# Forty-eight weight copies change their issuing engine, and one tile its place in a round of four

## The chip, the cores and the metric

The kernel runs on one core of a Trainium2 chip. The metric is the device time of one execution, in microseconds (us). Five engines work beside each other on a core, each with its own queue of instructions, done in order: TensorE (PE; PEld is its loading of weights), VectorE (DVE), ScalarE (ACT), GpSimd (POOL) and the sync engine (SP), which computes nothing and issues transfers. ACT and POOL can issue transfers too.

## The reference

A transformer trunk of two layers over 512 tokens of width 1024, all in float32:

```python
for layer in range(2):
    hn = rmsnorm(h, norm_mix[layer])
    if layer == 0: h = h + hybrid_attention(hn, ...)         # 8 grouped-query heads and 8 latent heads
    else:          h = h + neighbourhood_attention(hn, ...)  # 16 heads, an 8 x 16 window, a learned bias
    h = h + sq_relu_mlp(rmsnorm(h, norm_ffn[layer]), ffn_w_up[layer], ffn_w_down[layer])
return rmsnorm(h, final_norm)

def sq_relu_mlp(h, w_up, w_down):     # w_up 1024 x 4096, w_down 4096 x 1024
    u = relu(h @ w_up)
    return (u * u) @ w_down
```

## The kernel before

**Products.** Every float32 operand is split into a high part, rounded to a format that TensorE multiplies at its higher rate (`F32R`), and the rest, the low part. A product is three matmuls: high x high, high x low, low x high (`mm3`, L545 to L547). A weight chunk of 128 x 1024 is loaded by SP into half a raw tile (L214), ACT writes its high part `whi` (L236), and DVE the low part `wlo` (L226). `whi` and `wlo` have three buffers each. Chunks are loaded some 5 or 7 ahead of their use (`LOAD`) and split 2 ahead (`AHEAD`).

**The order of work.** The program is written as one stream. A planner then orders each engine's queue, by its own estimated times and with the place in the stream as priority; the order is fixed before the run. Three things bind it. `tc.keep_in_program_order(x)` puts `x` behind the instruction of the same engine that was written just before it. Inside `fixed_order()` (the second layer's attention) PE, ACT, DVE and POOL keep the written order, SP does not. And an instruction that must wait for data or for a free buffer holds up all that is behind it in its queue.

**The MLP.** `mlp_swept(l, made)` begins with `first_product`. It normalises `h`: for each of 8 blocks `hT[k]`, ACT and DVE write the high and low part of the scaled block (`split_g`, L551 and L552) and add its square to a sum (`sumsq_acc`, L559 on ACT, L561 on DVE). The first six tiles of `h @ w_up` are plain products: chunks 0 to 3 for four tiles, chunks 4 and 5 for two. The row norms are not needed before these end up in PSUM, so the norm's own matmuls (`compact_r`, L566) stand some steps into the product: after step 11 in the first layer, 13 in the second. Six chunks of `w_down` follow, and then the rest of `h @ w_up` by a scheme of seven products in place of eight for blocks of 2 x 2 (`Seven`, L416 to L418), whose weight sums POOL makes (`seven_chunk`, L326 to L331) and whose tiles are split at L336 and L337. The second product of the MLP goes by such a scheme as well (`Sweeps`, L1331 to L1449).

**Sums made ahead.** The sweeps need sums of blocks of `w_down`. `SumsAhead` makes them in device memory while earlier stages run: for each of 13 (first layer) or 11 (second) pairs of rows it copies two blocks of 512 KB from the weights to `made` (L841, issued by ACT), and POOL then adds blocks onto them with four accumulating transfers of 256 KB (L832). `steps()` is a generator; `tick` takes a step of it every few microseconds of planned TensorE work, from the latter part of the first attention (L1163), from the start of the second one (L1838) and through the MLP (`beat["every"]`). At the end of the up product `drain()` takes what is left.

**Raw tiles and the shared tile.** There are three raw tiles of 128 x 2048 (tag `raw`). In the MLP a fourth takes turns with them: the first 2048 columns of `shared`, whose 2560 columns otherwise hold five probability tiles of the attention (`p_tile`, 512 columns each, used in turn; the fifth is also `acc`, the sum of squares). `raw_pair()` hands out the next tile, as two halves for two chunks, or whole for a pair of `Seven`. `wide[0]` counts the place in the round, and 0 switches the shared tile off:

```python
        if wide[0]:
            wide[0] = wide[0] % 4 + 1
            if wide[0] == 1:
                return shared[:, 0:2048]
```

Before each MLP the attention's output projection runs (`out_proj`); its last chunks, five k-tiles first and three more after the last head in the second layer, lie in raw tiles. In the attention of the second layer ACT and POOL make the probabilities in `shared` (L1733, L1703) and PE transposes them from there (L1725); L1745 is the product with the values, L1714 the scores with their bias, which SP loads per head (L1778). L1004 adds the projection's tiles to `hT`.

Of the kernel before, what the change touches and what calls it, by code (L numbers as in the profile page):

```python
# [35 lines left out]
def encoder_kernel(ctx: ExitStack, tc: tile.TileContext, ins, out, dbg=None):  # L36
    nc = tc.nc
    PE, ACT, DVE, POOL, SP = nc.tensor, nc.scalar, nc.vector, nc.gpsimd, nc.sync
# [153 lines left out]
    wide = [0]  # L192
# [63 lines left out]
    LOAD = [5]  # L256
# [83 lines left out]
    class Seven:  # L340
# [27 lines left out]
        def split(self, kp, held=lambda z: z):  # L368

            for b in range(7):  # L370
                i = self.number(kp, b) // 2
                if i not in self.slots:
                    self.slots[i] = Slot()
            raw, t = self.raw.pop(kp)
            r, t_ = (s_.t.rearrange("p (b n) -> p b n", n=256) for s_ in (raw, t))
            b = 0
            while b < 7:
                q = self.number(kp, b)
                n = 2 if b in (3, 5) or (b < 2 and q % 2 == 0) else 1
                s_ = r[:, 1 + b : 1 + b + n] if b < 3 else t_[:, b - 3 : b - 3 + n]  # L380
                if n == 1:
                    d = self.at(kp, b)
                    hi, lo, s_ = d[:, 0], d[:, 1], s_[:, 0]
                else:
                    q = self.number(kp, b)
                    d = self.slots[q // 2].t.rearrange("p (q z n) -> p q z n", q=2, z=2)
                    hi, lo = d[:, :, 0], d[:, :, 1]
                ACT.activation(hi, s_, AF.Copy)
                held(DVE.tensor_tensor(lo, s_, f32(hi), op=ALU.subtract))
                b += n  # L390
                yield
            raw.free()
            t.free()
# [99 lines left out]
    def tiles(c0, n):  # L493
        return [(c0 + o, min(P, n - o)) for o in range(0, n, P)]
# [44 lines left out]
    def drain():  # L539
        for _ in beat["work"]:  # L540
            pass
# [279 lines left out]
    class SumsAhead:  # L821
# [12 lines left out]
        def steps(self):  # L834
            for kp in range(self.n + 3):
                if kp > self.n:
                    yield
                    yield
                if kp < self.n:
                    for z in range(2):  # L840
                        tc.keep_in_program_order(ACT.dma_start(self.made[kp, z], self.w[kp, z]))  # L841
                        yield
                for back, to, src, of in ((1, (1, 1), (0, 1), self.w), (1, (0, 1), (0, 0), self.w),
                                          (2, (0, 0), (1, 1), None), (3, (1, 0), (0, 0), None)):
                    if 0 <= kp - back < self.n:
                        self.add(kp - back, to, src, of)
                        yield
# [443 lines left out]
    def bias_rows():  # L1291
        held = tc.keep_in_program_order
        slot = Slot(F32)
        R, Fi, Fe = (slot.t[:, a:b] for a, b in ((0, 248), (248, 624), (624, 1008)))
        rpb = ins["od_rpb"][0]
        for qr in range(8):
            held(SP.dma_start(R[16 * qr : 16 * qr + 16],
                              rpb.rearrange("h a b -> h (a b)")[:, (7 - qr) * 31 : (7 - qr) * 31 + 248]))
            yield
        held(POOL.memset(Fi, NEG))  # L1300
        held(POOL.memset(Fe[:, 256:384], NEG))
        rv = R.rearrange("p (k d) -> p d k", d=31)
        held(POOL.tensor_copy(Fi.rearrange("p (j k) -> p j k", k=8)[:, 15:31, :], rv[:, 7:23, :]))
        held(POOL.tensor_copy(Fe[:, 0:248].rearrange("p (j k) -> p j k", k=8), rv))
        yield
        bxv = bx.rearrange("h t (c r) k -> t c r h k", r=8)
        for c in range(16):
            held(SP.dma_start(bxv[0, c].rearrange("r h k -> r h k"), Fi[:, (15 - c) * 8 : (15 - c) * 8 + 256]))
            yield

            v, off = (1, (7 - c) * 8) if c < 8 else (0, (23 - c) * 8)
            held(SP.dma_start(bxv[1, c][:, :, 128 * v : 128 * v + 128], Fe[:, off : off + 128]))
            yield
            held(SP.dma_start(bxv[1, c][:, :, 128 - 128 * v : 256 - 128 * v], Fe[:, 256:384]))
            yield
        slot.free()
# [35 lines left out]
    class Sweeps:  # L1352
# [66 lines left out]
        def run(self, R):  # L1419
# [33 lines left out]
            starts = {(0, 0), (0, 1), (1, 0), (2, 1)}  # L1453
            tail, held, waiting = [], {}, []
            for i, (kind, kp) in enumerate(steps):
                if i + 1 < len(steps):
                    ready_[steps[i + 1]] = self.tokens(*steps[i + 1])
# [50 lines left out]

    def mlp_swept(l, made, last=None):

        wide[0], LOAD[0] = 4, 7
        beat["every"] = (3.3, 3.6)[l]
        stage, ahead, later = first_product(l)
        w = ins["ffn_w_down"][l]
        bias = bias_rows() if l == 0 else iter(())
        U = stage(FIRST)[0]
        up = [s_.pair() for s_ in U]

        def ev(m, b):
            DVE.tensor_tensor(hT[:, m, :], hT[:, m, :], b, op=ALU.add)  # L1520

        gens = [product(w, 0, up, tiles(512 * c, 512), lambda j, b, c=c: ev(4 * c + j, b)) for c in range(2)]
        ahead()
        for c, gen in enumerate(gens):
            for i, _ in enumerate(gen):
                later(c, i)
                if i % 4 == 3 and c * 6 + i // 4 < 10:
                    next(bias, None)
        for s_ in U:
            s_.free()  # L1530
        reserve[0] = 3
        beat["every"] = (5.4, 7.0)[l]
        sweeps = []

        R = stage(0, RAW[l] + MORE[l], 0, lambda: sweeps.append(Sweeps(w, FIRST, made)))[1]
        R, more = R[: RAW[l] // 2], R[RAW[l] // 2 :]
        V = [Slot() for _ in range(MORE[l])]

        def split_more():
            for n, v in enumerate(V):  # L1540
                raw = more[n // 2]
                split(raw.t[:, S * (n % 2) : S * (n % 2) + S], v.pair())
                if n % 2:
                    raw.free()
                yield

        rest = split_more()
        drain()
        wide[0], LOAD[0] = 0, 5
        spare.clear()  # L1550
        reserve[0] = 6
        if last:
            beside = last(FIRST + RAW[l], V)
        else:
            beside = lambda kind, kp: None
            up = [s_.pair() for s_ in V]
            gens = [product(w, FIRST + RAW[l], up, tiles(512 * c, 512), lambda j, b, c=c: ev(4 * c + j, b))
                    for c in range(2) if up]
        for n, (kind, kp) in enumerate(sweeps[0].run(R)):
            beside(kind, kp)  # L1560
            if n % 16 == 15:
                next(rest, None)
            if kind and n % 5 == 0:
                next(bias, None)
        assert all(next(x, 0) == 0 for x in (rest, bias))
        reserve[0] = 1
        if not last:
            flip[0] = 1
            for gen in gens:
                for _ in gen:  # L1570
                    pass
            for s_ in V:
                s_.free()

    mlp_swept(0, ahead0)


# [276 lines left out]
    def last_mlp():  # L1854
# [80 lines left out]
        def last(k0, tiles_):  # L1935
# [10 lines left out]
            return beside  # L1946

        mlp_swept(1, ahead1, last)
        flip[0] = 1
        for run in runs:  # L1950
# [57 lines left out]
```

## Time and profile before

| | us |
|---|---|
| runs | 1174.4, 1178.94, 1178.77 (median 1178.77) |
| the profiled execution's own time | 1176.78 |
| its span | 1175.0 |
| busy: PE / DVE / ACT / POOL | 1145.0 / 917.2 / 673.8 / 467.3 |
| mean granted TensorE clock | 0.995 of full speed |

A line of the timeline has the start in the span, the duration, the engine, the line of the kernel, the operation, the tiles (written <- read), the shape, a count where neighbours are merged, and in brackets how long the engine was idle before it and what it waited for. SPq, ACTq and POOLq are the issuing of transfers by these engines' queues. A line of the chain that ended last has start, duration, and the work or the transfer that the chain went through. A row of a table of waits has who waited for whom, the total in us, how often, and the longest. Transfers issued by SP are queue q1 in the page, by ACT q10, by POOL q0; a row has packets, MB, and the packets' time as a share of 16 DMA engines over the span.

### The profile page before, as it was taken

How to read it: one execution, taken by the hardware profiler on the slowest of the kernel's cores; microseconds unless marked ns; L12 is line 12 of the kernel's file. 1: busy time of each engine (PE TensorE's matmuls, PEld its weight loads, DVE VectorE, ACT ScalarE, POOL GpSimd, SP SyncE). 2: the span in 40 equal slices, each digit the busy share in tenths (PEclk: the TensorE clock that was granted, in tenths of full speed). 3: DMA queues.
4: the chain of work that ended last, by engine and by line, in shares of the span. 5: the costliest groups of instructions: out<-in, count | busy, mean ns of one | idle time of the engine just before them, and what ended most of it. 6: DMA issues, size and time to landing. Idle time of an engine off the chain costs nothing.

```text
span 1175.0 us, 21065 instructions
## 1 busy us (share of the span) xinstructions
PE 1145.0 (97%) x7668; PEld 1033.8 (88%) x7668; DVE 917.2 (78%) x1627; ACT 673.8 (57%) x1157; POOL 467.3 (40%) x494
## 2 busy tenths in 40 slices
PE   9989999999999999999999999999899999999997
PEld 8667778888899999999998998988688999999995
DVE  5798988878878888998485666667796878799855
ACT  5468577564536657557454556545452665675625
POOL 3267354343878884000002243342285788400000
PEclk9999999999999999999999999999899999999998
DMA  7122478893776647867536498789467544565702
GB/s 272 55 80 83 134 188 210 185 231 125 168 173 170 152 119 209 272 192 252 184 107 162 130 264 226 189 208 253 161 132 188 133 122 116 161 208 180 250 2 71
DMA packets 131752, 197.32 MB, mean 168 GB/s; under 512 B 13012, under 2 KB 81537, under 8 KB 130881
## 3 DMA queue, kind: packets, MB, share of 16 engines
q1 hardware_dynamic: 113232, 138.18, 37.6%
q0 software_dynamic: 16128, 31.48, 16.3%
q10 hardware_dynamic: 2288, 26.32, 6.5%
q8 instruction: 60, 0.98, 0.4%
q14 instruction: 44, 0.35, 0.1%
HBM read 173.52 MB, written 56.62 MB: 196 GB/s over the span
## 4 chain that ended last, share of the span: by engine, by line
PE 77%; DVE 5%; DMA 5%; issue 1%; ACT 0%; POOL 0%; SPq 0%; DVEq 0%; ACTq 0%; POOLq 0%
PE mm L547 6%; PE mm L545 6%; PE mm L546 6%; PE mm L418 3%; PE mm L416 3%; PE mm L417 3%; PE t L1443 3%; PE t L1445 3%; PE t L1444 3%; DMA a<-a 2%; PE mm L1445 2%; PE mm L1443 2%; PE t L416 2%; PE mm L1444 2%; PE t L417 2%; PE t L418 2%
## 5 line engine op out<-in xcount | busy, mean ns | idle before, releaser
L545 PE MATMUL mm<-a,whi 128*128 128x512 f32 x395 | 160.9, 409 | 3.7 <-ACT whi L236 1.9
L547 PE MATMUL mm<-a,wlo 128*128 128x512 f32 x395 | 156.7, 399 | 0.3 <-DVE wlo L226 0.3
L546 PE MATMUL mm<-a,whi 128*128 128x512 f32 x395 | 156.6, 396 | 0.1
L337 DVE TENSOR_TENSOR wlo<-raw,whi 128x896 fp32r<-128x896 f32 x80 | 109.8, 1377 | 27.9 <-ACT whi L336 27.3
L336 ACT ACTIVATE whi<-raw 128x896 fp32r<-128x896 f32 x80 | 75.5, 950 | 87.0 <-PE o L546 27.5
L236 ACT ACTIVATE whi<-raw 128x1024 fp32r<-128x1024 f32 (+3 forms) x82 | 76.3, 933 | 75.6 <-PE s L546 26.9
L226 DVE TENSOR_TENSOR wlo<-raw,whi 128x1024 fp32r<-128x1024 f32 (+4 forms) x79 | 94.3, 1195 | 30.7 <-ACT whi L236 30.4
L545 PEld LDWEIGHTS mm<-a,whi 128*128 128x128 f32 x395 | 74.8, 189 | 20.2 <-ACT whi L236 3.0
L547 PEld LDWEIGHTS mm<-a,wlo 128*128 128x128 f32 x395 | 74.9, 190 | 17.3 <-DVE wlo L226 1.1
L546 PEld LDWEIGHTS mm<-a,whi 128*128 128x128 f32 x395 | 74.9, 190 | 13.2 <-DVE a L588 0.4
L1341 DVE TENSOR_TENSOR wlo<-a,whi 128x1024 fp32r<-128x1024 f32 x54 | 66.4, 1232 | 25.1 <-ACT whi L1340 25.0
L1611 POOL DMA_DIRECT2D a<-a x16 | 8.6, 542 | 182.0 <-PE mm L547 167.2
L1443 PE MATMUL t<-a,whi 128*128 128x256 f32 x288 | 80.8, 281 | 0.0
L1444 PE MATMUL t<-a,whi 128*128 128x256 f32 x288 | 80.8, 280 | 0.0
L1445 PE MATMUL t<-a,wlo 128*128 128x256 f32 x288 | 80.7, 280 | 0.0
L1078 POOL TENSOR_SCALAR shared<-shared,ti 128x512 f32<-128x512 f32 x64 | 47.2, 741 | 84.0 <-DVE ti L1077 64.9
L418 PE MATMUL mm<-a,wlo 128*128 128x256 f32 x280 | 78.8, 281 | 1.0 <-DVE wlo L337 1.0
L417 PE MATMUL mm<-a,whi 128*128 128x256 f32 x280 | 78.5, 281 | 0.0
L416 PE MATMUL mm<-a,whi 128*128 128x256 f32 x280 | 78.4, 280 | 0.0
L1340 ACT ACTIVATE whi<-a 128x1024 fp32r<-128x1024 f32 x54 | 56.9, 1054 | 37.4 <-PE t L1444 30.4
L1703 POOL TENSOR_SCALAR shared<-shared,ti 128x256 f32<-128x256 f32 x64 | 34.7, 557 | 92.3 <-DVE ti L1702 79.8
L330 POOL TENSOR_TENSOR raw<-raw 128x512 f32<-128x512 f32 x40 | 63.0, 1575 | 3.1
(399 smaller groups left out, 4028.4 us busy)
## 6 DMA issues: line engine op xcount, KB each, us to landing
made<-in_ffn_w_down_dram ACTq DMA_DIRECT2D x48, 512.0 KB
a<-made SPq DMA_DIRECT2D x86, 256.0 KB
raw<-in_ffn_w_up_dram SPq DMA_DIRECT2D x80, 256.0 KB
made<-in_ffn_w_down_dram POOLq DMA_DIRECT2D x48, 256.0 KB, 5.9
made<-made POOLq DMA_DIRECT2D x48, 256.0 KB, 6.0
raw<-in_ffn_w_down_dram SPq DMA_DIRECT2D x32, 256.0 KB
a<-in_ffn_w_down_dram SPq DMA_DIRECT2D x32, 256.0 KB
raw<-in_od_w_qkv_dram SPq DMA_DIRECT2D x64, 128.0 KB
```

Of the source, the lines that this page charges most:

```text
L226: z = lambda: (eng or DVE).tensor_tensor(to, src, f32(high), op=ALU.subtract)
L236: ACT.activation(hi[:, 0:m], raw[:, 0:m], AF.Copy)
L337: DVE.tensor_tensor(lo[:, 0:896], raw[:, 128:1024], f32(hi[:, 0:896]), op=ALU.subtract)
L416: PE.matmul(o, wh, x[:, 0], start=kp == 0 and n in (0, 1, 3, 5), stop=False, skip_group_check=True)
L417: PE.matmul(o, wh, x[:, 1], start=False, stop=False, skip_group_check=True)
L418: PE.matmul(o, wl, x[:, 0], start=False, stop=kp == self.np - 1, skip_group_check=True)
L545: PE.matmul(o, wh, xh, start=first, stop=False)
L546: PE.matmul(o, wh, xl, start=False, stop=False)
L547: PE.matmul(o, wl, xh, start=False, stop=last)
L1443: PE.matmul(o, wh, x[:, 0], start=first and m % 2 == 0, stop=False, skip_group_check=True)
L1444: PE.matmul(o, wh, x[:, 1], start=False, stop=False, skip_group_check=True)
L1445: PE.matmul(o, wl, x[:, 0], start=False, stop=last, skip_group_check=True)
```

## The change

The copies to `made` are issued by SP instead of ACT. And `wide[0]` starts at 1 instead of 4 in each MLP, so that the counter gives 2, 3, 4 and then 1: the shared tile is handed out fourth in each round, not first. The number of tiles, the chunks and their order, and all arithmetic stay.

```diff
@@ SumsAhead.steps
                 if kp < self.n:
                     for z in range(2):
-                        tc.keep_in_program_order(ACT.dma_start(self.made[kp, z], self.w[kp, z]))
+                        tc.keep_in_program_order(SP.dma_start(self.made[kp, z], self.w[kp, z]))
                         yield
@@ mlp_swept
-        wide[0], LOAD[0] = 4, 7
+        wide[0], LOAD[0] = 1, 7
         beat["every"] = (3.3, 3.6)[l]
```

## Prediction

> **What bounds the kernel now.** I read the page first, then the table of busy time in 25 us stretches, then the chain that ended last where that table shows a hole, and around the hole the timelines of PE, ACT, DVE and SP.
>
> ```profile
> PE 1145.0 (97%) x7668; PEld 1033.8 (88%) x7668; DVE 917.2 (78%) x1627; ACT 673.8 (57%) x1157; POOL 467.3 (40%) x494
> ```
>
> TensorE is the bound: 30 us of 1175.0 are not PE time. An edit that adds or removes no matmul can win only where PE is idle, or where its clock is low.
>
> ```profile
> 775.00:800.00 25.00, 24.95 (x137) 21.14 (x136) 17.45 (x48) 12.23 (x33) 8.93 (x13) 1.00 0.82 226
> 800.00:825.00 25.00, 23.97 (x115) 19.00 (x114) 18.39 (x30) 13.33 (x22) 6.04 (x8) 1.00 1.02 272
> 825.00:850.00 25.00, 20.38 (x81) 16.38 (x80) 17.67 (x31) 9.52 (x15) 4.32 (x3) 0.86 0.40 139
> 850.00:875.00 25.00, 25.00 (x110) 20.36 (x109) 22.76 (x21) 17.57 (x30) 21.61 (x20) 1.00 0.63 137
> ```
>
> The first number behind the stretch's length is PE's busy time; the last three are granted clock, DMA share and GB/s. The hole lies at 823 us, where the second MLP begins. PE is idle for 50 - 23.97 - 20.38 = 5.65 us there, and the clock of 0.86 costs (1 - 0.86) x 25 = 3.5 us more. Just ahead of it the DMA engines are full (1.02). PE's timeline splits the hole in two:
>
> ```profile
> 823.96 0.50 PE L545 MATMUL mm<-a,whi 128*128 128x512 f32 x1 [0.83 <-ACT whi L236]
> 824.30 0.39 PE L546 MATMUL mm<-a,whi 128*128 128x512 f32 x1
> 824.53 0.39 PE L545 MATMUL mm<-a,whi 128*128 128x512 f32 x1
> ...
> 830.71 0.55 PE L566 MATMUL t<-ones,shared 128*128 128x1 f32 x3 [4.62 <-DVE shared L561]
> ```
>
> 0.83 us go on the high part of the first up-weight chunk (L236), 4.62 us on the last step of the sum of squares (L561), in all 5.45. Both lead back to one place on ACT:
>
> ```profile
> 817.96 0.61 ACT L559 ACTIVATE sc<-hT 128x512 f32<-128x512 f32 x1
> 822.85 2.01 ACT L236 ACTIVATE whi<-shared 128x1024 fp32r<-128x1024 f32 x2 [4.28 <-DMA shared<-in_ffn_w_up_dram]
> 824.76 0.71 ACT L551 ACTIVATE a<-hT,gT 128x512 fp32r<-128x512 f32 x1
> ...
> 828.77 0.61 ACT L559 ACTIVATE sc<-hT 128x512 f32<-128x512 f32 x1
> ```
>
> ACT waits 4.28 us for the load into `shared`, and behind it in ACT's order stand the four pairs L551/L559 that DVE's L552/L561 need. The chain shows why the load is late:
>
> ```profile
> 804.40 0.45 PE t L1725 x4
> ...
> 804.91 17.84 DMA shared<-in_ffn_w_up_dram
> ```
>
> SP may start it only when PE has transposed the last probabilities, which lie in the same tile; it then took 17.84 us, behind other transfers.
>
> **Edit 1: the shared tile comes fourth in the round (`wide[0]` 1 instead of 4).** `raw_pair` steps `wide[0]` before it tests it. So now the first pair of up chunks (0 and 1) takes `shared`, chunks 2 to 5 two raw tiles, down chunks 0 and 1 the third. After the edit chunks 0 to 5 take the three raw tiles, and down chunks 0 and 1 take `shared`. It is the same ring of four, shifted. SP's issues show when each tile came free:
>
> ```profile
> 798.62 0.37 SPq L214 DMA_DIRECT2D shared<-in_ffn_w_up_dram  x1
> 801.18 3.06 SPq L214 DMA_DIRECT2D raw<-in_ffn_w_up_dram  x3
> 804.91 0.37 SPq L214 DMA_DIRECT2D shared<-in_ffn_w_up_dram  x1
> 805.33 0.73 SPq L214 DMA_DIRECT2D raw<-in_ffn_w_up_dram  x1
> 813.31 4.50 SPq L214 DMA_DIRECT2D raw<-in_ffn_w_down_dram  x2
> ```
>
> The last two probability tiles of the attention are `shared[0:1024]`, the place of chunk 0, so 804.91 is chunk 0 and 798.62 is chunk 1. After the edit chunk 0 gets the raw tile of 801.18, 3.73 us earlier and ahead of the loads that now precede it. Even with the same 17.84 us it would land at 801.18 + 17.84 = 819.02. ACT's four earlier pairs end at 817.96 + 0.61 = 818.57, so L236 starts at about 819 at worst instead of 822.85, and PE, which ends the output projection at about 823.1, does not wait: 0.83 us gained.
>
> What is late next is the sum of squares. Its pairs need `hT`:
>
> ```profile
> 821.11 0.69 DVE L1004 TENSOR_TENSOR hT<-hT,s 128x512 f32<-128x512 f32 x1 [0.98 <-PE s L547]
> 821.80 1.38 DVE L1004 TENSOR_TENSOR hT<-hT,t 128x512 f32<-128x512 f32 x2
> 823.17 0.69 DVE L1004 TENSOR_TENSOR hT<-hT,o 128x512 f32<-128x512 f32 x1
> ...
> 829.97 0.69 DVE L561 TENSOR_TENSOR shared<-shared,sc 128x512 f32<-128x512 f32 x1
> ```
>
> The first is there at 821.80. ACT's four pairs, which now run from 824.76 to 829.38, can start about 2.9 us earlier, so the last L561 ends near 830.66 - 2.9 = 827.8. Meanwhile PE has work: the norm's matmuls (L566) stand after 14 steps of the product, each three matmuls at 0.23 us (the starts at 824.30 and 824.53), 14 x 0.69 = 9.7 us, until about 832.8. PE reached them early only because the low part of chunk 0 (L226) was missing and the planner put L566 ahead of L547. With L236 done by 820.1, DVE can do L226 in the 0.98 us ahead of 821.11 at the price of pushing L1004 by some tenths. So the 4.62 us go too. The first MLP has this picture already: its load into `shared` is no wait for ACT and PE has no gap there.
>
> With the gap the low clock goes:
>
> ```profile
> 73.75 0.73 PE L1070 MATMUL s<-a,a 128*128 128x512 f32 x2 [2.39 <-DVE ti L1074]
> ```
>
> This gap of 2.39 us left the clock at full speed, the one of 4.62 us did not; so any rest below 2.4 us keeps it. [...]
>
> Edit 1 gives 0.83 + 4.62 + 3.5 = 8.95 us. Its other effects I take at nothing. Chunks 4 and 5 are issued at 813.31 instead of 805.33; PE needs chunk 4 after four chunks of 8 x 0.69 = 5.5 us, at 823.1 + 22 = 845, so 17.84 us of landing fit, with 14 to spare. In the first MLP the ring moves in the same way, under PE that is never idle there. Bounds: 0 (the rivals) and 8.95.
>
> **Edit 2: 48 copies of 512 KB move from ACT's queue to SP's.**
>
> ```profile
> L841 ACTq DMA_DIRECT2D made<-in_ffn_w_down_dram x48: 496/496/852, 130.3 to 894.5; - x48
> ```
>
> ACT loses 48 x 0.496 = 23.8 us of issuing. ACT is 57% busy and, beyond the hole above, no PE gap from 210 us to the end is over 0.6 us, so I take this as 0. SP gains as much; it mostly waits. [...]
>
> What remains is order. A copy waits for no data; it is pinned only behind the SP transfer traced before it, and so goes out earlier than now rather than later, and may stand ahead of loads in one queue.
>
> ```profile
> q10 hardware_dynamic: 2288, 26.32, 6.5%
> ```
>
> ACT's queue (q10) moved 26.32 MB in 6.5% of the span, so one copy (0.524 MB) is 0.065 x 1175 x 0.524 / 26.32 = 1.5 us of all 16 engines. At the hole it matters like this:
>
> ```profile
> 811.95 0.50 ACTq L841 DMA_DIRECT2D made<-in_ffn_w_down_dram  x1
> ```
>
> Two copies issued there would go out before 801, ahead of chunk 0: at most 3.0 us, 819.0 + 3.0 = 822.0, still ahead of 823.1. In the first layer's attention five waits of the chain are for SBUF to SBUF transfers from SP, the first and the last of which are
>
> ```profile
> 141.16 5.50 DMA a<-a
> ...
> 205.40 5.67 DMA a<-a
> ```
>
> A copy in front of each would cost 5 x 1.5 = 7.5 us at most. At best the moves gain the 0.5 us that PE idles for them at 156.3. Copies stand among these transfers today as well (205.18 in the last wait), so I take half a copy: 0.8 us lost.
>
> **The sum.** 1176.78 - 8.95 + 0.8 = 1168.6 us against the profiled execution's own 1176.78 (span 1175.0). That execution lies 2.0 us below the median of 1178.77, inside the runs' 1174.4 to 1178.94. The mean of these four is 1177.2, and from there I get 1169.1; I say 1169.5.
>
> **Rivals.** First, the hole is shortened, not closed. If the planner leaves L226 behind the eight L552/L561, PE does eight matmuls (1.9 us) from 823.1 and waits from 825.0 to 827.8. Then 0.83 + 1.8 us are gained, and the clock's 3.5 us or not: 1171 to 1174.5. For it: that is DVE's order today. Against: today L236 comes so late that DVE had no other choice; in the first MLP L226 stands ahead of these.
>
> Second, edit 1 wins and edit 2 gives it back: the five transfers above each get a whole copy in front, 8.95 - 7.5 = 1.5 us left, 1175.3. For it: PE's order is fixed before the run, so a late transfer stalls it. Against: PE idles only 0.5 us for them now and has other work around.
>
> Third, slower: SP holds the copies up. SP issues in order, and a load that waits for its tile holds what is behind it:
>
> ```profile
> SPq L1778 <- DVE ti L1714: 55.5, 12, 10.8
> ```
>
> POOL's accumulating transfers (L832) wait for the copies, and POOL's scaling of the probabilities stands behind them:
>
> ```profile
> 679.91 0.50 ACTq L841 DMA_DIRECT2D made<-in_ffn_w_down_dram  x1
> ...
> 688.39 0.86 POOL L832 DMA_DIRECT2D made<-in_ffn_w_down_dram  x1
> ```
>
> The first pair has 8.5 us; later pairs have the planned two copies and up to four additions between. It decides when a copy comes over 8.5 - 1.5 = 7 us late. With waits of up to 10.8 us each stall costs up to 3.8 us; four of them, and edit 1 lost to the same queue, give 1176.8 + 15 = 1192; with edit 1 kept, 1183. Against it: a copy traced behind a load is mostly issued early, as SP runs ahead.
>
> **How the numbers follow.** Forecast 0.52, first rival 0.20, second 0.15, third 0.13. Half a per cent is about 5.9 us, what a measurement of this kernel can tell from no change; below 1172.9 is faster, above 1184.7 slower. Faster takes nine tenths of the forecast and a third of the first rival, 0.54; slower nearly all of the third rival, 0.12; the rest, 0.34, is the same. The likeliest case alone reaches from 1164 (runs that start at 1174.4, the full 8.95 and the 0.5 at 156 and a little of ACT's) to 1173. Taking in the second rival with some room for a few stalls of its kind, and leaving the third out, 1164 to 1181 leaves out about 0.18.
>
> **What would show it.** Right: around 815 to 830 us ACT's first L236 of the second MLP reads `raw`, with no wait for a DMA; L566 comes after some 14 steps, without a gap; the stretch after 825 has a clock of 1.00; DMA issues by ACT shrink to the constants and the output, and q10 to a few MB. Wrong: a PE gap over 2.4 us at the same place; new PE gaps at 140 to 215 us behind DMA a<-a; POOL's L832 waiting for `made`; in the first MLP a gap where up chunks 4 and 5 come late.

## The result and the profile after

The changed kernel takes 1167.52 us (median of 6 runs, 1165.67 to 1169.0), the kernel before beside it 1178.86 (6 runs, 1174.4 to 1182.38): a ratio of 0.9901, 95% interval 0.9883 to 0.992. It is faster by 11.3 us. The profiled execution took 1167.6, with a span of 1165.8; the one of before took 1176.78.

The page after, busy times and the two transfer queues of SP (q1) and ACT (q10):

```profile
PE 1141.2 (98%) x7668; PEld 1032.8 (89%) x7668; DVE 912.2 (78%) x1627; ACT 674.7 (58%) x1157; POOL 464.3 (40%) x494
...
q1 hardware_dynamic: 114768, 163.35, 43.6%
...
q10 hardware_dynamic: 752, 1.15, 0.4%
```

The 25 MB of copies have left ACT's queue; ACT's and POOL's busy times change by less than 1%. The table of stretches shows the hole at the start of the second MLP gone, with a clock of 1.00 where it was 0.86, and a new low clock at 50 to 100 us (1.00 in both stretches before):

```profile
50.00:75.00 25.00, 18.88 (x80) 12.43 (x79) 20.78 (x45) 13.57 (x25) 13.56 (x9) 0.98 0.36 110
75.00:100.00 25.00, 24.91 (x145) 20.43 (x143) 20.81 (x53) 19.86 (x45) 16.48 (x18) 0.95 0.16 37
800.00:825.00 25.00, 24.55 (x118) 19.83 (x117) 20.44 (x34) 15.30 (x28) 7.11 (x8) 1.00 1.03 282
825.00:850.00 25.00, 25.00 (x116) 20.56 (x115) 23.12 (x37) 12.32 (x21) 10.15 (x10) 1.00 0.29 91
```

The timeline of the changed kernel at the same place, ACT, DVE and PE:

```profile
819.23 1.04 ACT L236 ACTIVATE whi<-raw 128x1024 fp32r<-128x1024 f32 x1
...
820.21 0.68 DVE L561 TENSOR_TENSOR shared<-shared,sc 128x512 f32<-128x512 f32 x1
820.82 1.21 DVE L226 TENSOR_TENSOR wlo<-raw,whi 128x1024 fp32r<-128x1024 f32 x1
821.95 0.68 DVE L1004 TENSOR_TENSOR hT<-hT,s 128x512 f32<-128x512 f32 x1
...
829.01 0.68 DVE L561 TENSOR_TENSOR shared<-shared,sc 128x512 f32<-128x512 f32 x1
...
831.18 0.95 PE L566 MATMUL t<-ones,shared 128*128 128x1 f32 x8
```

ACT no longer waits for a load, and PE no longer waits at L566. But there is a third difference. DVE now takes the low part of chunk 0 (L226) ahead of the last four L1004. In the kernel before, DVE's timeline has it behind the last L561:

```profile
829.97 0.69 DVE L561 TENSOR_TENSOR shared<-shared,sc 128x512 f32<-128x512 f32 x1
830.57 2.36 DVE L226 TENSOR_TENSOR wlo<-shared,whi 128x1024 fp32r<-128x1024 f32 x2
```

In the prediction the early load brought the early L226. The experiments ask whether that is so.

### The profile page after: what moved, and what is told of

It is laid out like the page before. It is cut to its first block, busy times and chain, and to the rows that moved or that the text cites. A ratio compares the mean times of both kernels' runs of the same rounds, so it can differ in the third digit from the quotient of the medians.

```text
span 1165.8 us, 21085 instructions
## 1 busy us (share of the span) xinstructions
PE 1141.2 (98%) x7668; PEld 1032.8 (89%) x7668; DVE 912.2 (78%) x1627; ACT 674.7 (58%) x1157; POOL 464.3 (40%) x494
## 4 chain that ended last, share of the span: by engine, by line
PE 81%; DVE 4%; ACT 1%; issue 1%; DMA 1%; POOL 0%; SPq 0%; DVEq 0%; ACTq 0%; POOLq 0%
PE mm L545 6%; PE mm L547 6%; PE mm L546 6%; PE t L1443 3%; PE t L1445 3%; PE t L1444 3%; PE mm L418 3%; PE mm L416 3%; PE mm L417 3%; PE mm L1445 2%; PE mm L1443 2%; PE mm L1444 2%; PE t L416 2%; PE t L417 2%; PE t L418 2%; PE s L1070 2%
## 5 line engine op out<-in xcount | busy, mean ns | idle before, releaser
L547 PE MATMUL mm<-a,wlo 128*128 128x512 f32 x395 | 155.9, 396 | 0.3 <-DVE wlo L226 0.3
L337 DVE TENSOR_TENSOR wlo<-raw,whi 128x896 fp32r<-128x896 f32 x76 | 100.3, 1330 | 52.6 <-ACT whi L336 52.6
L236 ACT ACTIVATE whi<-raw 128x1024 fp32r<-128x1024 f32 (+3 forms) x86 | 80.4, 938 | 72.3 <-PE s L546 21.3
L226 DVE TENSOR_TENSOR wlo<-raw,whi 128x1024 fp32r<-128x1024 f32 (+4 forms) x83 | 94.8, 1146 | 29.8 <-ACT whi L236 29.8
L336 ACT ACTIVATE whi<-raw 128x896 fp32r<-128x896 f32 x76 | 70.9, 945 | 52.6 <-PE o L417 18.7
L547 PEld LDWEIGHTS mm<-a,wlo 128*128 128x128 f32 x395 | 74.3, 189 | 16.7 <-DVE wlo L226 0.8
L1388 ACT ACTIVATE a<-a 128x512 fp32r<-128x512 f32 (+1 forms) x96 | 46.4, 515 | 28.5 <-DVE wlo L1341 25.8
```

The costliest lines, as they stand in the source:

```text
L226: z = lambda: (eng or DVE).tensor_tensor(to, src, f32(high), op=ALU.subtract)
L236: ACT.activation(hi[:, 0:m], raw[:, 0:m], AF.Copy)
L337: DVE.tensor_tensor(lo[:, 0:896], raw[:, 128:1024], f32(hi[:, 0:896]), op=ALU.subtract)
L547: PE.matmul(o, wl, xh, start=False, stop=last)
```

## Experiments

Each ratio is to the kernel before on the same chip in the same set of runs (medians of 1178.67, 1178.91 and 1178.32 us in the three sets).

### The two edits apart

The tile alone:

```diff
-        wide[0], LOAD[0] = 4, 7
+        wide[0], LOAD[0] = 1, 7
```

> The tile's new place alone; ScalarE still issues the copies. Theory (the gain is the hole at the start of the second MLP, opened by chunk 0's late load into the shared tile): the hole of 5.45 us idle and 3.5 us low clock closes, ratio to before 0.990 to 0.9935, no PE gap over 1 us between 800 and 850 us, first L236 of the second MLP from raw with no DMA wait. Rival (the moved copies do it, by leaving the DMA engines free while chunk 0 is in flight): ratio 0.997 to 1.001, the hole stays.

The copies alone:

```diff
-                        tc.keep_in_program_order(ACT.dma_start(self.made[kp, z], self.w[kp, z]))
+                        tc.keep_in_program_order(SP.dma_start(self.made[kp, z], self.w[kp, z]))
```

> The copies alone; the shared tile is still first in the round. Theory: chunk 0 is still released only at about 805 us, the hole stays at least in part, ratio 0.996 to 1.002. Rival (moved copies do it): two copies that were issued at 811.95 us go out before chunk 0's load, it lands well under 17.84 us after its issue, the hole closes, ratio 0.990 to 0.9935.

The tile alone gave 1175.45 us, 0.9972 (0.9959 to 0.9985). The copies alone gave 1168.31 us, 0.9905 (0.9889 to 0.9921): as much as both. Timelines of the tile alone:

```profile
821.85 1.04 ACT L236 ACTIVATE whi<-raw 128x1024 fp32r<-128x1024 f32 x1
...
824.47 0.69 DVE L1004 TENSOR_TENSOR hT<-hT,s 128x512 f32<-128x512 f32 x1 [0.97 <-PE s L547]
...
832.20 3.48 DVE L226 TENSOR_TENSOR wlo<-raw,whi 128x1024 fp32r<-128x1024 f32 x3
832.33 1.87 PE L566 MATMUL t<-ones,shared 128*128 128x1 f32 x8 [3.98 <-DVE shared L561]
```

ACT finds chunk 0 landed and has its high part at 822.9. DVE then stands idle for 0.97 us, until 824.47, with that high part there, and takes the low part only at 832.20, behind the eight L552/L561; PE still waits 3.98 us. Timelines of the copies alone:

```profile
821.91 2.01 ACT L236 ACTIVATE whi<-shared 128x1024 fp32r<-128x1024 f32 x2 [2.25 <-DMA shared<-in_ffn_w_up_dram]
823.00 1.23 DVE L226 TENSOR_TENSOR wlo<-shared,whi 128x1024 fp32r<-128x1024 f32 x1 [1.78 <-ACT whi L236]
824.14 0.68 DVE L1004 TENSOR_TENSOR hT<-hT,s 128x512 f32<-128x512 f32 x1
...
831.73 1.05 PE L566 MATMUL t<-ones,shared 128*128 128x1 f32 x8
```

Here ACT still waits for the load into `shared`, and the hole is closed all the same: L226 stands ahead of L1004, and L566 follows without a gap. So the late load is not what made the long gap. The ratio is the one that the rival of this run named, but not by its mechanism: SP issues the pair at 807.08, behind chunk 0's load (806.00), and ACT has that load only at 821.91, some 15.9 us after its issue.

### The load early in another way, and the steps kept away

In the second attention the probability tiles are turned by two places, so that chunk 0's half of `shared` comes free first; copies and round as before:

```diff
+        turn_p[0] += 2
         prev = ripe = None
         for n in range(16):
```

> The kernel before, but the turn of the probability tiles is moved on by two at the start of the second attention, so that its last head uses shared[1024:2048] (chunk 1) and not shared[0:1024] (chunk 0). The shared tile stays first. Theory (it is the release of chunk 0's place that is late): chunk 0's load is issued near 798.6 us, chunk 1's near 805; ACT's first L236 waits less than 1.5 us instead of 4.28, the gap before L566 shrinks below 2.5 us, ratio 0.991 to 0.996. Rival (DMA engines are full, any load issued around 800 lands at 820): ACT waits over 3 us as before, ratio 0.998 to 1.002.

1177.99 us, 0.9996 (0.9983 to 1.0008). Timelines:

```profile
819.21 1.05 ACT L236 ACTIVATE whi<-shared 128x1024 fp32r<-128x1024 f32 x1
...
830.75 2.35 DVE L226 TENSOR_TENSOR wlo<-shared,whi 128x1024 fp32r<-128x1024 f32 x2
830.89 1.87 PE L566 MATMUL t<-ones,shared 128*128 128x1 f32 x8 [5.16 <-DVE shared L561]
```

The load is early by another way, and the gap is as long as ever, with L226 last again.

Then the generator of the copies rests from step 13 of the second attention until the first tiles of the MLP are staged. All copies stay on ACT, but none is issued around the hole:

```diff
+        if n == 13:
+            beat["rest"] = True
@@ mlp_swept
         U = stage(FIRST)[0]
         up = [s_.pair() for s_ in U]
+        beat["rest"] = False
```

> The kernel before, with the making of the sums (copies and additions) paused from head 13 of the second attention until the first six tiles of the up product are done; same work, later. Theory (release late and queue full, both needed for the hole): chunk 0's load, still issued near 805 us, lands in under 10 us, by 815, ACT does not wait for it, the hole closes, ratio 0.990 to 0.995, unless the late sums hold up the sweeps. Rival (release alone): the load is issued as late as before and the hole stays, ratio 0.998 to 1.002.

1169.62 us, 0.9924 (0.9908 to 0.994). Timeline of DVE:

```profile
822.82 1.21 DVE L226 TENSOR_TENSOR wlo<-shared,whi 128x1024 fp32r<-128x1024 f32 x1
823.95 0.68 DVE L1004 TENSOR_TENSOR hT<-hT,s 128x512 f32<-128x512 f32 x1
```

The hole is closed with the tile first and the copies on ACT. By itself this run doesn't tell order from traffic: the DMA share from 800 to 825 us is 0.51 here, against 1.02 before. In all six kernels the place of L226 in DVE's queue and the long gap go together. So does a pair of copies issued by ACT 6 to 11 us ahead of L236; the tile's place and the landing of the load do not. The new theory, argued so far: the hole is an order that the planner wrote before the run. It counts the issuing of a copy on ACT as time of ACT. The eighth pair of the second layer (at 811.95 us in the kernel before) stands in ACT's order ahead of four pairs L551/L559 and of L236, makes L236 late in the plan, and L226 goes behind the sum of squares.

### One pair of copies, forwards and backwards

In the kernel before, that pair alone goes to SP; in the changed kernel, that pair alone goes back to ACT:

```diff
-                        tc.keep_in_program_order(ACT.dma_start(self.made[kp, z], self.w[kp, z]))
+                        eng = SP if self.n == 11 and kp == 7 else ACT    # the other: ACT if ... else SP
+                        tc.keep_in_program_order(eng.dma_start(self.made[kp, z], self.w[kp, z]))
```

> The kernel before, with one of the 24 pairs of copies moved: the eighth pair of the second layer, whose two issues stood on ScalarE at 811.95 us, goes to SP; the other 46 copies stay on ScalarE and the shared tile stays first in the round. Theory of the order (the hole at 823 us comes from the planned order of VectorE, L226 of the first up chunk behind the eight L552/L561, and that order comes from the pair of issues that the planner puts on ScalarE just ahead of L236): this pair alone closes the hole though the load into shared still lands as late; no PE gap over 1 us between 815 and 850, clock 1.00 in 825:850, ratio to before 0.989 to 0.9935. Rival (the copies only added traffic or ScalarE's 23.8 us of issuing count as a whole): one pair of 24 gives a twenty-fourth of the gain, ratio 0.998 to 1.001, and the gap of 4 to 5 us at L566 stays.

> The changed kernel, with that one pair (second layer, eighth) put back on ScalarE; 46 copies on SP, the shared tile fourth. Theory of the order: VectorE takes the first L226 behind the eight L552/L561 again, PE waits 3.5 to 5 us at L566 near 830 us and the clock of 825:850 falls to about 0.86, ratio to before 0.996 to 1.000 as with the tile's part alone (0.9972). Rival (the other 46 issues or the tile's place in the round close the hole): ratio 0.989 to 0.993, no gap.

The pair alone on SP: 1170.25 us, 0.9932 (0.9917 to 0.9948). The stretch, and the timeline of ACT and DVE:

```profile
825.00:850.00 25.00, 24.97 (x115) 20.30 (x115) 23.07 (x38) 12.74 (x18) 6.20 (x5) 1.00 0.52 181
```

```profile
825.04 2.01 ACT L236 ACTIVATE whi<-shared 128x1024 fp32r<-128x1024 f32 x2 [1.85 <-DMA shared<-in_ffn_w_up_dram]
826.13 1.23 DVE L226 TENSOR_TENSOR wlo<-shared,whi 128x1024 fp32r<-128x1024 f32 x1 [1.38 <-ACT whi L236]
827.27 0.68 DVE L1005 TENSOR_TENSOR hT<-hT,s 128x512 f32<-128x512 f32 x1
```

One pair of 24 closes the hole, though chunk 0's load is still waited for. That it does so is shown; that the planner's time for ACT is the reason is the likeliest reading, no more. The pair alone back on ACT: 1173.47 us, 0.9959 (0.9942 to 0.9975), just under the range expected, and the hole is there again, though chunk 0 reads `raw` without a wait:

```profile
828.05 3.49 DVE L226 TENSOR_TENSOR wlo<-raw,whi 128x1024 fp32r<-128x1024 f32 x3
828.19 1.75 PE L566 MATMUL t<-ones,shared 128*128 128x1 f32 x8 [3.99 <-DVE shared L561]
```

### The order alone

Nothing is edited but the place of L226 of that one chunk. In the changed kernel it is held to its traced place, behind the eight L552/L561; in the kernel before its priority is raised (`pinned` is set in the second MLP's `plain()`; both edits shortened):

```diff
+                ins = (eng or DVE).tensor_tensor(to, src, f32(high), op=ALU.subtract)
+                if pinned:
+                    pinned.pop()
+                    tc.keep_in_program_order(ins)
```

```diff
+                if pinned:
+                    pinned.pop()
+                    with tc.high_priority():
+                        (eng or DVE).tensor_tensor(to, src, f32(high), op=ALU.subtract)
```

> The changed kernel with nothing altered but the place of one instruction: L226 of the first up chunk of the second MLP is held to the order in which it is traced on VectorE, which puts it behind the eight L552/L561. All 48 copies stay on SP and the tile is fourth. Theory of the order: the hole comes back, a PE gap of 3.5 to 5 us at L566 near 830 us with a clock near 0.86 after it, ratio to before 0.995 to 1.000. Rival (queues and landings of the transfers make the gain, the order only follows from them): ratio 0.989 to 0.993, no gap over 1 us there.

> The kernel before with nothing altered but the place of one instruction: L226 of the first up chunk of the second MLP gets a higher priority, so that the planner puts it ahead of the four L1004 and the eight L552/L561. All 48 copies stay on ScalarE and the tile is first. Theory of the order: that alone closes the hole, no PE gap over 1.5 us from 815 to 850, clock 0.99 to 1.00 in 825:850, ratio to before 0.989 to 0.9945. Rival (the late load is the cause, as the prediction had it, or ScalarE's issuing is): L236 still waits for the load into shared near 822 us, PE still idles over 3 us, ratio 0.997 to 1.001.

Pinned late: 1174.53 us, 0.9964 (0.995 to 0.9978). With the added lines L228 is the subtraction, L571 what was L566:

```profile
831.01 3.49 DVE L228 TENSOR_TENSOR wlo<-raw,whi 128x1024 fp32r<-128x1024 f32 x3
831.15 1.76 PE L571 MATMUL t<-ones,shared 128*128 128x1 f32 x8 [3.90 <-DVE shared L566]
```

Raised: 1171.77 us, 0.9953 (0.9934 to 0.9973); its own range for the order alone reached to 0.9945. Here L231 is the raised subtraction, L243 was L236, L554 was L547 and L573 was L566:

```profile
824.26 2.01 ACT L243 ACTIVATE whi<-shared 128x1024 fp32r<-128x1024 f32 x2 [3.16 <-DMA shared<-in_ffn_w_up_dram]
825.35 1.23 DVE L231 TENSOR_TENSOR wlo<-shared,whi 128x1024 fp32r<-128x1024 f32 x1 [2.69 <-ACT whi L243]
826.63 0.51 PE L554 MATMUL mm<-a,wlo 128*128 128x512 f32 x1 [0.51 <-DVE wlo L231]
...
834.09 1.05 PE L573 MATMUL t<-ones,shared 128*128 128x1 f32 x8 [0.20 <-DVE shared L568]
```

With the engine of every copy and the place of every tile as they were, the place of one DVE instruction takes the long gap away or brings it back. The planner moved a little else with it: pinned, one L557 goes ahead of the last L1009 on DVE; raised, ACT makes the high part of chunk 2 ahead of its last four pairs. Neither touches chunk 0. Now, and only now, the late load costs something: small gaps, 0.79 us in all from 815 to 850 us. So the tile was added to the raised order, copies still on ACT (`wide[0]` 1 as well):

> The kernel before with L226 of the second MLP's first up chunk raised and the shared tile fourth; all 48 copies stay on ScalarE. With the order alone raised (0.9953) PE still lost 1.3 us at 826 us, since L236 waited 3.16 us for the late load. If the tile's place is worth what that wait costs once the order is right: L236 of that chunk reads raw without waiting for a DMA, no PE gap over 0.3 us from 815 to 850, ratio 0.9925 to 0.9945. If the place is worth nothing even then: 0.995 to 0.9965.

1169.93 us, 0.992 (0.99 to 0.9939), just below the range of the first case. ACT's L243 (was L236) reads `raw` at 822.89 without a wait, PE has no gap there, and the ratio lies 0.0033 below that of the order alone. That is some 3.9 us, more than the 0.79 us of gaps, and the two intervals overlap a little, so the tile's price is not settled.

### The first layer's copies

The pair alone gives 0.9932, all copies 0.9905. The profile of the pair alone had one long gap more, in the first layer's attention, where PE's timeline and the chain that ended last say:

```profile
159.22 1.65 PE L1071 MATMUL s<-a,a 96*128 96x512 f32 x3 [3.63 <-DMA a<-a]
```

```profile
147.96 3.01 DMA a<-a
150.99 8.18 DMA a<-a
```

With it the clock was at half speed for 6.8 us by the trace's clock records, which no other kernel with the first layer's copies on ACT shows. Added to the pair on SP, the first layer's 26 copies:

```diff
+                        eng = SP if self.n != 11 or kp == 7 else ACT
+                        tc.keep_in_program_order(eng.dma_start(self.made[kp, z], self.w[kp, z]))
```

> The kernel before with the second layer's eighth pair on SP, as in the run with that pair alone (0.9932), and with the first layer's 26 copies on SP as well; the second layer's other 20 copies stay on ScalarE, the tile first. Open is the rest between that pair alone (0.9932, where PE waited 3.63 us for a transfer a<-a at 159 us and the clock then lost 3.4 us) and all 48 copies (0.9905). If the rest lies in the first layer, where ScalarE's copies stand ahead of the transfers a<-a: no PE gap behind DMA a<-a from 140 to 215 us, ratio 0.9885 to 0.992. If it lies in the second layer's other copies, or was chance: ratio 0.992 to 0.995.

1166.06 us, 0.9889 (0.9872 to 0.9907): under the pair alone with room between the intervals, some 5 us. In the seven profiles with the first layer's copies on ACT, PE waits 0.48 to 3.63 us for a transfer `a<-a` between 156 and 160 us; in the six with them on SP it never waits there for a transfer. On ACT a copy is issued 0.1 to 1.2 us ahead of that transfer in all seven (150.85 and 150.98 in the kernel before). On SP the planner puts copies elsewhere, as in SP's timeline of this kernel (L842 the copies, L961 the transfer):

```profile
151.57 1.26 SPq L961 DMA_DIRECT2D a<-a  x2
154.18 0.51 SPq L842 DMA_DIRECT2D made<-in_ffn_w_down_dram  x1
```

DVE's and PE's order changed in this stage too, so how much of the 5 us is the queue and how much the order stays open. The second layer's other 20 copies make no difference that can be told (0.9889 without them, 0.9905 with them).

### The clock at 74 us

The changed kernel loses 25 x (0.02 + 0.05) = 1.75 us to low clock in the stretches from 50 to 100 us above, behind a PE gap of 2.37 us that ends at 74.04. Eight matmuls without use were written behind the first two score products of the first attention:

```diff
+        warm, warm_b = [4, 4], ob()
...
                 p = scores(h, i)
+                if warm:
+                    idle_work(warm.pop(), warm_b)
```

> The changed kernel with eight matmuls more that compute nothing used, behind the first two products of queries and keys in the first attention, in the gap of 2.37 us that PE has at 74 us; their result is not read. Theory of the clock: that gap sets off the 3.4 us at half clock which six of the profiles show at 74 to 78 us; filled, the clock stays at 1.00 there, 1.7 us are won in the runs that had it, ratio 0.9875 to 0.990 against 0.9901 of the changed kernel. Rival (the low clock there does not come from the gap, or the matmuls delay the first products as much): the clock in 75:100 stays 0.95, or the ratio is 0.990 to 0.9925.

1164.32 us, 0.9873 (0.9856 to 0.9889), the lowest median of all kernels run, though its interval overlaps that of the changed kernel. But not as expected. Stretches and PE's timeline:

```profile
50.00:75.00 25.00, 20.85 (x98) 14.13 (x97) 20.56 (x51) 14.20 (x28) 13.36 (x10) 1.00 0.31 89
75.00:100.00 25.00, 22.88 (x138) 18.88 (x139) 22.23 (x52) 20.53 (x47) 15.89 (x18) 1.00 0.29 82
```

```profile
60.73 0.38 PE L144 MATMUL o<-ones 128*128 128x128 f32 x2
...
61.51 1.05 PE L144 MATMUL o<-ones 128*128 128x128 f32 x8
62.84 0.94 PE L144 MATMUL o<-ones 128*128 128x128 f32 x6
...
71.77 0.74 PE L1071 MATMUL s<-a,a 128*128 128x512 f32 x2 [0.15 <-DVE ti L1075]
```

The planner put the matmuls (two records each in the trace) at 61 to 64 us, not into the gap. The order of DVE's queue changed again: the scaling factors that the scores' next step waits for (L753) are made at 70.62 instead of 72.89. The scores came 2.27 us earlier (71.77 instead of 74.04), the long gap was not filled but gone, and the clock stayed at 1.00. Clock and order are not separated by this run.

## Why the prediction was right in its number and wrong in its cause

- **What the hole costs (8.95 us): right.** The gaps of 0.83 and 4.62 us and the low clock of 825 to 850 us are gone together. One misplaced instruction brings the long gap and the low clock back (a gap of 3.90 us and a clock of 0.86; 0.9901 to 0.9964, 7.4 us).
- **Edit 1 closes the hole: wrong, the step that failed.** Its first half came as written: L236 reads `raw` at 819.23 with no wait, against the 819 worked out. The failed inference is the next one, that DVE then does L226 ahead of L1004 because it can: in the run with edit 1 alone DVE does it last, at 832.20, and PE waits 3.98 us. DVE does what the planner wrote, and the planner does not know when the load lands. Edit 1 alone gave 0.9972, about 3.3 us, of which the shorter gaps at the hole explain 1.5. The prediction stated the true mechanism twice, as "the planner put L566 ahead of L547" and as the first rival, and set it aside because the measured L236 was late.
- **Edit 2: 0 for ACT, 0.8 us lost in SP's queue: mis-sized, and with the wrong sign.** It alone gives 0.9905, 11.2 us: one pair, through the order, 0.9932 (8.0 us), and the first layer's copies some 5. The prediction counted the issues as 23.8 us of ACT's own time, as if no order hung on them; the pair alone shows that one does. The bound on the first layer was wrong as well: it allowed 0.5 us for PE's wait there, from the one execution shown, while the other six profiles with these copies on ACT have 0.75 to 3.63 us, the longest with a loss of clock besides.
- **When the norm's matmuls come: a size off, harmless.** L566 was put at about 832.8, after 14 steps, and came at 831.18, after 12, four of them without their low product, because chunk 1's L226 (829.61) still stands behind the last L561; the last L561 was put near 827.8 and ended at 829.01 + 0.68 = 829.7. The order still holds, with 1.5 us to spare instead of 5.
- **The sum.** 1168.6 us for the profiled execution, 1167.6 came. The agreement is partly chance: the true loss at the hole was booked to the wrong edit, the first layer's gain was missing, and the 1.75 us of clock lost at 74 us were not foreseen.
- **"Any rest below 2.4 us keeps the clock": wrong**: in the changed kernel a gap of 2.37 us is followed by 3.41 us at half clock, see the last section.
- **The rivals.** The second, copies in front of the transfers `a<-a`, named the right place with the sign turned: it is with the copies on ACT that PE waits there, and whether they are what holds the transfers up stays open. The third, SP holding copies up, did not come: in the trace after, no PE gap of 0.15 us or more behind POOL is left after 61.5 us.

Open: why the planner's own figures tip at that pair (its estimates are in no trace), and how queue and order share the first layer's 5 us.

## What to carry to other kernels

Where queues are ordered before the run from estimated times, an edit is two edits: what it does to the work, and what it does to the plan. Compare the order of the instructions on each engine around the bottleneck before looking at landings: if the critical one is late in its queue while its inputs are long there, no earlier transfer helps, and raising that one instruction tells in a single run. Split an edit before believing its story, even when its time came out as forecast.

## What the runs showed of the hardware that was not expected

The gap at 74 us measures 2.37 to 2.39 us in twelve profiles and is followed by 3.4 us at half clock in eight of them; in four, the kernel before among them, it is not. Here are the gap and the windows of 2 us of the changed kernel; the two matmuls behind the gap take 1.22 us, against 0.73 in the kernel before:

```profile
74.04 1.22 PE L1070 MATMUL s<-a,a 128*128 128x512 f32 x2 [2.37 <-DVE ti L1074]
```

```profile
72.00:74.00 2.00, 0.00 (x0) 0.00 (x0) 1.71 (x8) 0.57 (x1) 0.00 (x0) 0.97 0.82 309
74.00:76.00 2.00, 1.96 (x5) 1.58 (x6) 2.00 (x5) 1.52 (x4) 0.00 (x0) 0.50 0.00 0
76.00:78.00 2.00, 2.00 (x8) 1.57 (x7) 0.89 (x5) 1.44 (x3) 0.48 (x1) 0.68 0.00 0
```

In the trace's clock records every low stretch ahead of the one in which the execution ends begins and ends a whole number of 3.4133 us after the clock first reached full speed: 826.03 us (242 times that) and 832.85 us (244) in the kernel before, 68.27 us (20) and 71.68 us (21) in the changed one. No stretch of that grid was idle throughout at this gap: by the grid of each profile, the gap filled at most 1.92 to 2.39 us of one stretch in the eight, and at most 1.52 to 1.89 us in the four. So in these twelve profiles the same gap comes with a loss of 1.7 us (half of 3.4) or with none by where it falls on the grid, and the grid begins anywhere from 3.9 to 6.9 us into the span. A single profile's clock says little of such a gap. No run moved the gap on the grid on purpose.
